# Chunk mask of the prompt attention: from separate one-row matmuls to two extra contraction rows

## The chip, the cores and the metric

The kernel runs on one core of a Trainium2 chip. The metric is the device time of one execution in microseconds (us). The kernel before takes 1581.94 us, the median of three runs (1581.4 to 1583.57).

## The reference

One layer of a streaming encoder on 1024 prompt positions and 8 x 16 sample positions. The change lies in the attention of the prompt (8 heads, 96 query and key values per head, chunks of 64 positions):

```
key_chunk = jnp.arange(S) // CHUNK                 # CHUNK = 64
q_chunk = (i * Q_BLOCK + jnp.arange(Q_BLOCK)) // CHUNK
s = jnp.einsum('bqhd,bkhd->bhqk', qi, k).astype(jnp.float32) * ATTN_SCALE
mask = key_chunk[None, :] <= q_chunk[:, None]
s = jnp.where(mask[None, None], s, NEG_INF)        # NEG_INF = -1e30
pr = jax.nn.softmax(s, axis=-1).astype(v.dtype)
return jnp.einsum('bhqk,bkhd->bqhd', pr, v)
```

Around it stand the input projection, the attention of the sample with its cache, a state-space layer, the output projection and a gated feed-forward part with a depthwise convolution. The S5, sample and feed-forward parts are not touched.

## The kernel before

All products are float32 made of pairs: an operand is split into a high part (written as float32r by ScalarE) and a low part (the rest, by VectorE or GpSimd), and `mm3` at L132 issues three matmuls, high by high, low by high and high by low.

The prompt attention is `phase_c` (L1120). The 1024 positions are four groups `j` of 256, each of two halves `z` of 128; the eight heads are two groups `g` of four. A stage is one (j, g), in the order j = 0, 1, 3, 2. The parts of a stage are generators that are advanced step by step:

- `back(i)` makes the keys of 128 positions: scale, transposes `ptk`, the split into `kh` and `kl` (tiles `kT[j]`). `kh` has 97 rows: 96 of the key and one row of ones, which a DMA on GpSimd's queue (L1159) brings from the array `one`.
- `prep(j, g)` (L1182) loads the queries from DRAM into `qnl`, transposes them into `ptq` and splits them into `qh` (97 rows) and `ql`. Both come from the pool of eight slots with the tag `L` (`wk`, L769), which they share with `cTh`, `cTl` (inputs of the projections of the next 128 positions), `O` (output of the attention) and the weights `ws`, `wh`, `wl`.
- `rowmax(j, g)` (L1196) finds the maximum of each query: matmuls of the high parts into `psm` (L1214), a reduction `mx` on VectorE (L1218), a transpose `pm`, and a copy of the negated maximum into row 96 of `qh` (L1227, ScalarE).
- `attn(j, g)` (L1232) takes one head and one `j` of the keys a step: three matmuls for each half of the keys into `pst` (L1247 with all 97 rows, so that the maximum is subtracted by the product; L1248; L1249), exponential `pf` (L1254), split into `ph` and `pl` (L1256, every third `pl` on GpSimd), and three matmuls each into `po` (L1260 to L1262).

Only the diagonal (keys of the same `j`) needs a mask: in each block of 128 by 128, the first 64 queries must not see the last 64 keys. Before, a further matmul adds -1e30 there. It has one contraction row in bfloat16, 128 stationary columns of `sel` (zeros and ones) and 64 moving columns of `neg`, at L1216 in `rowmax` and at L1251 in `attn`:

```
nc.tensor.matmul(p_[:, u, n - 64:n], lhsT=sel[:, 0], rhs=neg, start=False, stop=True)
nc.tensor.matmul(o_[:, 0:64], lhsT=sel[:, 1], rhs=neg, start=False, stop=True)
```

Each of the two lines issues 64 matmuls (8 stages, 4 heads, 2 halves). Four memsets on VectorE (L1134 to L1137) fill `sel` and `neg`.

`step` (L1319) interleaves the steps of `rowmax` and `attn`; the loop at L1330 mixes them with the projections (`middle`, `front`) of the later positions, and `phase_de` with the loads and the first matmuls `pw` of the output projection. Within this program order the framework writes the order of each engine's instructions itself (L1703, `schedule_with_timeline_sim=True`), from its own model of durations, and gives out the slots of the pools; only a part of the feed-forward has PE's order written by hand (L1582). On the chip every engine then runs its list in that order.

Of the kernel before, what the change touches and what calls it, by code (L numbers as in the profile page):

```python
# [10 lines left out]
F32R = mybir.dt.float32r  # L11
BF16 = mybir.dt.bfloat16
# [5 lines left out]
P = 128  # L18
# [9 lines left out]
H = 8  # L28
# [2 lines left out]
RD = 32  # L31
QN = 64
QD = QN + RD
NATW = QL + KL + RD
SW = 512
DIN = NATW + SW
# [16 lines left out]
NEG = -1e30  # L53
# [21 lines left out]
def build(tc, t):  # L75
    nc = tc.nc
# [3 lines left out]
    with root:  # L80
# [688 lines left out]
        def wk(tag, shape, name, dt=F32, rows=P):  # L769
            n = 1  # L770
            for z in shape:
                n *= z
            sz, bufs = {"L": (1024, NL), "M": (512, NM)}[tag]
            x = cst["W"].tile([P, sz], dt, tag=tag, name=name, bufs=bufs)[0:rows, 0:n]
            if len(shape) > 1:
                ax = "abcdef"[:len(shape)]
                x = x.rearrange("p (%s) -> p %s" % (" ".join(ax), " ".join(ax)), **dict(zip(ax[1:], shape[1:])))
            return x
# [341 lines left out]
        def phase_c():  # L1120
# [3 lines left out]
            kT, V = {}, {}  # L1124
            cst["V"] = V
            sc = cst["cw"]
            cs_ = cst["W"]
# [1 line left out]
            load(gq, t["g_qh"])  # L1129
            load(gk, t["g_kh"])  # L1130
            stt(gq, gq, SCALE, gk, ALU.mult, ALU.mult)
            sel = cs_.tile([1, 2, P], BF16, name="sel")
            neg = cs_.tile([1, 64], BF16, name="neg")
            nc.vector.memset(neg, NEG)  # L1134
            nc.vector.memset(sel, 0.0)
            nc.vector.memset(sel[:, 0, 0:64], 1.0)
            nc.vector.memset(sel[:, 1, 64:P], 1.0)  # L1137
            for j in range(4):
                es = ExitStack()
                kv = es.enter_context(tc.tile_pool(name=f"kv{j}", bufs=1, **R))  # L1140
                kvs.append(es)
                kT[j] = [kv.tile([QD + 1 - n, H, 2 * P], F32R, name=f"k{'hl'[n]}{j}") for n in range(2)]
                V[j] = [kv.tile([P, 2, H, QN + 1 - n], F32R, name=f"v{n}{j}") for n in range(2)]
                nc.gpsimd.memset(V[j][0][:, :, :, QN:QN + 1].bitcast(F32), 1.0)
            aps = ExitStack()
# [6 lines left out]
            def back(i):  # L1152
                j, z = i // 2, i % 2
                tsl = slice(i * P, (i + 1) * P)
                zs = slice(z * P, (z + 1) * P)
                kh, kl = kT[j]
                kn, qs, rr = pj.pop(i)
                if z == 0:
                    nc.gpsimd.dma_start(out=kh[QD:QD + 1].rearrange("p h q -> p (h q)"), in_=t["one"].bitcast(F32R))  # L1159
                rq = rr[:, 0].rearrange("p (h o) -> p h o", o=1)  # L1160
                rk = rr[:, 1].rearrange("p (h o) -> p h o", o=1)
                mul(kn[:, :, QN:QD], kpe[:, i:i + 1].to_broadcast([P, H, RD]), rk.to_broadcast([P, H, RD]), nc.gpsimd)
                for g in range(2):
                    h4 = slice(4 * g, 4 * g + 4)
                    mul(kn[:, h4, 0:QN], kn[:, h4, 0:QN], rk[:, h4].to_broadcast([P, 4, QN]))
                    pt = psum(TG[4] if i not in TE else TGE[2], [QD, 4, P], "ptk")
                    for h in range(4):
                        nc.tensor.transpose(pt[:, h], kn[:, 4 * g + h], ident)
                    split(kh[0:QD, h4, zs], kl[:, h4, zs], pt)
                cr = sc.tile([P, H, 16], F32, tag="cr", name="cr")  # L1170
                sr = sc.tile([P, H, 16], F32, tag="sr", name="sr")
                mul(cr, cosb[:, i:i + 1].to_broadcast([P, H, 16]), rq.to_broadcast([P, H, 16]), nc.gpsimd)
                mul(sr, sinb[:, i:i + 1].to_broadcast([P, H, 16]), rq.to_broadcast([P, H, 16]), nc.gpsimd)
                for g in range(2):
                    h4 = slice(4 * g, 4 * g + 4)
                    rope(sc, qs[g][:, :, QN:QD].rearrange("p h (a d) -> p h a d", a=2), qs[g][:, :, QN:QD], cr[:, h4], sr[:, h4], "rp", nc.gpsimd)
                    mul(qs[g][:, :, 0:QN], qs[g][:, :, 0:QN], rq[:, h4].to_broadcast([P, 4, QN]), nc.gpsimd)
                    store(q_dram[tsl, g * 4 * QD:(g + 1) * 4 * QD].rearrange("p (h d) -> p h d", d=QD), qs[g])
# [1 line left out]
            qT = {}  # L1180

            def prep(j, g):  # L1182
                qh = wk("L", [4, 2 * P], "qh", F32R, QD + 1)
                ql = wk("L", [4, 2 * P], "ql", F32R, QD)
                qT[j, g] = (qh, ql)
                for z in range(2):
                    zs = slice(z * P, (z + 1) * P)
                    qn = wk("M", [4, QD], "qnl")
                    i = 2 * j + z
                    load(qn, q_dram[i * P:(i + 1) * P, g * 4 * QD:(g + 1) * 4 * QD].rearrange("p (h d) -> p h d", d=QD))  # L1190
                    pt = psum(TG[5 if not pos["post"] else 10], [QD, 4, P], "ptq")
                    for h in range(4):
                        nc.tensor.transpose(pt[:, h], qn[:, h], ident)
                    split(qh[0:QD, :, zs], ql[:, :, zs], pt, gq)

            def rowmax(j, g):  # L1196
                qh, _ = qT[j, g]
                nb = j // 2 + 1
                mx = cs_.tile([P, 4, 2, 2], F32, tag="mx", name="mx", bufs=2)
                nm = cs_.tile([P, 4, 2], F32, tag="nmx", name="nmx", bufs=2)  # L1200
                for c in range(2):
                    for h in (2 * c, 2 * c + 1):
                        for z in range(2):
                            lh = qh[0:QD, h, z * P:(z + 1) * P]
                            for hb in range(nb):
                                tot = 0
                                p_ = psum(TG[6], [P, 2, 2 * P], "psm")
                                for u in range(2):
                                    jj = 2 * hb + u
                                    if jj > j:  # L1210
                                        break
                                    n = P if jj == j and z == 0 else 2 * P
                                    dg = jj == j
                                    nc.tensor.matmul(p_[:, u, 0:n], lhsT=lh, rhs=kT[jj][0][0:QD, 4 * g + h, 0:n], start=True, stop=not dg)  # L1214
                                    if dg:
                                        nc.tensor.matmul(p_[:, u, n - 64:n], lhsT=sel[:, 0], rhs=neg, start=False, stop=True)  # L1216
                                    tot += n
                                nc.vector.tensor_reduce(out=mx[:, h, z, hb:hb + 1], in_=p_.rearrange("p a k -> p (a k)")[:, 0:tot],  # L1218
                                                        axis=AX.X, op=ALU.max)
                                if (h % 2, z, hb) != (1, 1, nb - 1):  # L1220
                                    yield
                    nc.vector.tensor_reduce(out=nm[:, 2 * c:2 * c + 2], in_=mx[:, 2 * c:2 * c + 2, :, 0:nb], axis=AX.X, op=ALU.max, negate=True)
                    pm = psum(TG[7], [1, 2, 2, P], "pm")
                    for hh in range(2):
                        for z in range(2):
                            nc.tensor.transpose(pm[:, hh, z], nm[:, 2 * c + hh, z:z + 1], ident)
                    acopy(qh[QD:QD + 1, 2 * c:2 * c + 2], pm.rearrange("p h z q -> p h (z q)"))  # L1227
                    yield
# [3 lines left out]
            def attn(j, g):  # L1232
                qh, ql = qT.pop((j, g))
                O = wk("L", [4, 2 * P], "O", rows=QN + 1)
                for h in range(4):
                    po = psum("y", [QN + 1, 2 * P], "po")
                    for jj in range(j + 1):
# [6 lines left out]
                        for z, (sc_, qs_) in enumerate(cols):  # L1244
                            ks = slice(z * P, (z + 1) * P)
                            o_ = p_[:, sc_]
                            nc.tensor.matmul(o_, lhsT=kh[:, 4 * g + h, ks], rhs=qh[:, h, qs_], start=True, stop=False)  # L1247
                            nc.tensor.matmul(o_, lhsT=kl[:, 4 * g + h, ks], rhs=qh[0:QD, h, qs_], start=False, stop=False)  # L1248
                            nc.tensor.matmul(o_, lhsT=kh[0:QD, 4 * g + h, ks], rhs=ql[:, h, qs_], start=False, stop=not dg)  # L1249
                            if dg:  # L1250
                                nc.tensor.matmul(o_[:, 0:64], lhsT=sel[:, 1], rhs=neg, start=False, stop=True)  # L1251
                        pf = wk("M", [4 * P], "pf")
                        ph, pl = [cst["ap"].tile([P, 4 * P], F32R, tag=x_, name=x_) for x_ in ("ph", "pl")]
                        nc.scalar.activation(out=pf[:, 0:n], in_=p_[:, 0:n], func=AF.Exp)  # L1254
# [368 lines left out]
def arrays(inp):  # L1623
# [3 lines left out]
    o = {}  # L1627
    x = np.concatenate([a["x_prompt"].reshape(SEQ, DM), a["x_sample"].reshape(NB * DSEQ, DM)], 0)
    o["xT"] = c(x.T)
    o["one"] = np.ones((1, 2 * P * H), f)  # L1630
    o["ident"] = np.eye(P, dtype=f)
    pos = np.concatenate([np.arange(SEQ), np.tile(PAST + np.arange(DSEQ), NB)]).astype(f)
    inv = (f(10000.0) ** (-np.arange(0, RD, 2, dtype=f) / f(RD))).astype(f)
# [91 lines left out]
```

## Time and profile before

| | |
|---|---|
| median of the timed runs | 1581.94 us |
| span of the profiled execution | 1582.0 us (the page gives no other time of it) |
| PE busy | 1497.2 us (95%) |
| PE weight loads busy | 1427.5 us (90%) |
| VectorE (DVE) busy | 1119.5 us (71%) |
| ScalarE (ACT) busy | 683.8 us (43%) |
| GpSimd (POOL) busy | 320.6 us (20%) |
| mask matmuls, L1216 and L1251 | 64 each, 435.6 to 656.7 us |

PE is TensorE's matmul row, PEld its weight loads. The duration of a matmul in the profile holds its passage through the array, so that matmuls that follow each other overlap in the rows; what one takes of the engine is the distance between its start and the start of the next.

### The profile page before, as it was taken

Reading aid. Unit: us, or ns where it says so; the run is one execution under the profiler, and the core shown is the slowest. Engines: PE = TensorE matmul, PEld = TensorE weight load, DVE = VectorE, ACT = ScalarE, POOL = GpSimd, SP = SyncE. Lnnn points to the kernel's source line nnn. Section 1 sums busy time; section 2 is a strip of 40 time slices with the busy share of each in tenths; the row PEclk is TensorE's granted clock in tenths of the full one; section 3 lists DMA queues with packets and bytes.
Section 4 is the critical chain, followed back from the end, with each engine's and each line's share of the span. In section 5 each row is a group of like instructions: output and inputs, shape, how many; then the busy total and the mean of one; then the engine's idle time right before and its main releaser. Section 6 shows DMA issues by size and latency. Waiting matters only on the chain.

```text
span 1582.0 us, 24076 instructions
## 1 busy us (share of the span) xinstructions
PE 1497.2 (95%) x8861; PEld 1427.5 (90%) x8861; DVE 1119.5 (71%) x2376; ACT 683.8 (43%) x1323; POOL 320.6 (20%) x616
## 2 busy tenths in 40 slices
PE   7896857999999999999999999999999999999998
PEld 6876745877888898999999999999999999999998
DVE  8983799485777676367676766776766777777766
ACT  6442346666666676434433333333333333333321
POOL 3550466130444222112100000000100000000000
PEclk9998867999999999999999999999999999999999
DMA  7449343463321222451021111111111111111103
GB/s 203 122 144 161 114 154 57 111 186 97 97 69 48 78 65 65 151 165 52 1 84 37 41 41 41 50 45 40 41 41 41 46 49 51 44 41 40 41 1 130
DMA packets 101205, 122.00 MB, mean 77 GB/s; under 512 B 39240, under 2 KB 81416, under 8 KB 100624
## 3 DMA queue, kind: packets, MB, share of 16 engines
q1 hardware_dynamic: 100960, 120.44, 27.1%
q8 instruction: 69, 1.13, 0.3%
q14 instruction: 48, 0.39, 0.1%
q0 software_dynamic: 128, 0.03, 0.0%
HBM read 93.79 MB, written 26.65 MB: 76 GB/s over the span
## 4 chain that ended last, share of the span: by engine, by line
PE 80%; DVE 11%; DMA 4%; ACT 2%; issue 1%; SPq 1%; POOL 0%; DVEq 0%; ACTq 0%
PE pu L137 35%; PE pd L137 16%; PE pw L137 6%; DVE w L104 3%; PE pk L137 3%; PE pst L1247 2%; PE pg L137 1%; PE pq L137 1%; PE psm L1214 1%; PE pst L1248 1%; PE po L1260 1%; PE po L1262 1%; PE pst L1249 1%; PE pS L137 1%; PE po L1261 1%
## 5 line engine op out<-in xcount | busy, mean ns | idle before, releaser
L104 DVE TENSOR_TENSOR hT<-hT,pd 128x384 f32<-128x384 f32 x528 | 288.2, 551 | 211.7 <-PE pd L137 211.6
L137 PE MATMUL pu<-hnh,wl 128*128 128x384 f32 x1056 | 353.9, 335 | 0.0
L137 PE MATMUL pu<-hnl,wh 128*128 128x384 f32 x1056 | 353.9, 335 | 0.0
L137 PE MATMUL pu<-hnh,wh 128*128 128x384 f32 x1056 | 353.6, 335 | 0.0
L137 PE MATMUL pd<-act,wh 128*128 128x384 f32 x1056 | 348.0, 336 | 0.5 <-DVE hT L104 0.4
L1532 ACT ACTIVATE c<-pu,cvh 128x384 f32<-128x384 f32 x132 | 88.7, 672 | 302.1 <-PE pu L137 302.0
L137 PEld LDWEIGHTS pd<-act,wh 128*128 128x128 f32 x1056 | 197.7, 188 | 2.4 <-DVE hT L104 2.3
L137 PEld LDWEIGHTS pu<-hnh,wh 128*128 128x128 f32 x1056 | 198.2, 188 | 0.0
L137 PEld LDWEIGHTS pu<-hnl,wh 128*128 128x128 f32 x1056 | 198.2, 188 | 0.0
L137 PEld LDWEIGHTS pu<-hnh,wl 128*128 128x128 f32 x1056 | 198.0, 187 | 0.0
L122 DVE SCALAR_TENSOR_TENSOR c<-u,cvh,c 128x256 f32<-128x256 f32 (+1 forms) x352 | 171.1, 516 | 26.8 <-ACT u L101 13.8
L137 PE MATMUL pd<-act,wl 128*128 128x384 f32 x528 | 178.3, 338 | 0.0
L101 ACT ACTIVATE act<-c 128x384 fp32r<-128x384 f32 x66 | 34.7, 526 | 158.8 <-DVE c L104 158.8
L137 PEld LDWEIGHTS pd<-act,wl 128*128 128x128 f32 x528 | 99.2, 188 | 0.0
L1538 POOL COPY u<-u 128x2 f32<-128x2 f32 x88 | 20.0, 228 | 379.1 <-DVE c L104 172.1
L104 DVE TENSOR_TENSOR wl<-ws,wh 128x1024 fp32r<-128x1024 f32 x74 | 91.0, 1234 | 6.0 <-ACT wh L101 6.0
L101 ACT ACTIVATE wh<-ws 128x1024 fp32r<-128x1024 f32 x74 | 78.0, 1057 | 11.7 <-PE pw L137 6.5
L1550 POOL COPY cvo<-u 128x2 f32<-128x2 f32 x44 | 8.1, 184 | 353.9 <-ACT u L101 353.9
L1218 DVE TENSOR_REDUCE mx<-psm 128x1 f32<-128x512 f32 (+2 forms) x96 | 52.3, 550 | 29.8 <-PE psm L1216 15.0
L1554 ACT ACTIVATE c<-c 128x384 f32<-128x384 f32 x66 | 34.7, 526 | 75.1 <-DVE c L122 75.0
L101 ACT ACTIVATE u<-pu 128x384 f32<-128x384 f32 (+2 forms) x176 | 66.2, 404 | 0.0
L137 PE MATMUL pw<-oh,wh 128*128 128x384 f32 x192 | 64.9, 339 | 0.0
(468 smaller groups left out, 3174.6 us busy)
## 6 DMA issues: line engine op xcount, KB each, us to landing
ws<-in_w_up SPq DMA_DIRECT2D x44, 512.0 KB, 3.7
ws<-in_w_down SPq DMA_DIRECT2D x22, 512.0 KB, 3.6
xs<-in_xT SPq DMA_DIRECT2D x24, 192.0 KB, 3.5
os<-o_dram SPq DMA_DIRECT2D x24, 192.0 KB, 2.7
hT<-in_xT SPq DMA_DIRECT2D x24, 192.0 KB, 4.3
out_yT<-hT SPq DMA_DIRECT2D x24, 192.0 KB, 2.1
cf<-in_cT SPq DMA_DIRECT2D x8, 512.0 KB, 4.7
cn<-in_cn SPq DMA_DIRECT2D x8, 512.0 KB, 7.1
```

The source lines that it names most:

```text
L101: nc.scalar.activation(out=out, in_=in_, func=AF.Copy, scale=scale)
L104: (eng or nc.vector).tensor_tensor(out=out, in0=a, in1=b, op=op)
L122: nc.vector.scalar_tensor_tensor(out=out, in0=a, scalar=s, in1=b, op0=op0, op1=op1)
L137: nc.tensor.matmul(out, lhsT=w, rhs=x, start=first and i == 0, stop=last and i == n - 1)
L1214: nc.tensor.matmul(p_[:, u, 0:n], lhsT=lh, rhs=kT[jj][0][0:QD, 4 * g + h, 0:n], start=True, stop=not dg)
L1218: nc.vector.tensor_reduce(out=mx[:, h, z, hb:hb + 1], in_=p_.rearrange("p a k -> p (a k)")[:, 0:tot], axis=AX.X, op=ALU.max)
L1247: nc.tensor.matmul(o_, lhsT=kh[:, 4 * g + h, ks], rhs=qh[:, h, qs_], start=True, stop=False)
L1248: nc.tensor.matmul(o_, lhsT=kl[:, 4 * g + h, ks], rhs=qh[0:QD, h, qs_], start=False, stop=False)
L1249: nc.tensor.matmul(o_, lhsT=kh[0:QD, 4 * g + h, ks], rhs=ql[:, h, qs_], start=False, stop=not dg)
L1532: nc.scalar.activation(out=c, in_=p_, func=AF.Identity, scale=w[2], bias=w[3])
L1538: nc.gpsimd.tensor_copy(out=u[:, 0:2], in_=halo[i, gv][:, TB:TB + 2])
L1554: nc.scalar.activation(out=g_, in_=g_, func=AF.Silu)
```

## The change

The constant row of the keys becomes three rows, and the queries get two rows more, so that the product of the two new pairs of rows is -1e30 for the masked combinations and 0 elsewhere. The tiles `kh` and `qh` have 99 rows (`QM`). Rows 96 to 98 of `kh` come by the same DMA on GpSimd's queue from the array `kmask` (3 x 2048 instead of 1 x 2048 values). For `qh`, each `prep` issues a new DMA on GpSimd's queue from `qmask` (3 x 1024 values) into rows 96 to 98; row 96 is zero until `rowmax` writes the negated maximum there. On the diagonal, `rowmax` and the first matmul of `attn` contract 99 rows; elsewhere they contract 96 and 97 as before. The matmuls with `sel` and `neg`, these tiles and their memsets are gone.

```diff
+QM = QD + 3
-            sel = cs_.tile([1, 2, P], BF16, name="sel")
-            neg = cs_.tile([1, 64], BF16, name="neg")
-            nc.vector.memset(neg, NEG)
-            nc.vector.memset(sel, 0.0)
-            nc.vector.memset(sel[:, 0, 0:64], 1.0)
-            nc.vector.memset(sel[:, 1, 64:P], 1.0)
...
-                kT[j] = [kv.tile([QD + 1 - n, H, 2 * P], F32R, name=f"k{'hl'[n]}{j}") for n in range(2)]
+                kT[j] = [kv.tile([(QM, QD)[n], H, 2 * P], F32R, name=f"k{'hl'[n]}{j}") for n in range(2)]
...
-                    nc.gpsimd.dma_start(out=kh[QD:QD + 1].rearrange("p h q -> p (h q)"), in_=t["one"].bitcast(F32R))
+                    nc.gpsimd.dma_start(out=kh[QD:QM].rearrange("p h q -> p (h q)"), in_=t["kmask"].bitcast(F32R))
...
-                qh = wk("L", [4, 2 * P], "qh", F32R, QD + 1)
+                qh = wk("L", [4, 2 * P], "qh", F32R, QM)
+                nc.gpsimd.dma_start(out=qh[QD:QM].rearrange("p h q -> p (h q)"), in_=t["qmask"].bitcast(F32R))
...
-                                    nc.tensor.matmul(p_[:, u, 0:n], lhsT=lh, rhs=kT[jj][0][0:QD, 4 * g + h, 0:n], start=True, stop=not dg)
-                                    if dg:
-                                        nc.tensor.matmul(p_[:, u, n - 64:n], lhsT=sel[:, 0], rhs=neg, start=False, stop=True)
+                                    r = QM if dg else QD
+                                    nc.tensor.matmul(p_[:, u, 0:n], lhsT=qh[0:r, h, z * P:(z + 1) * P], rhs=kT[jj][0][0:r, 4 * g + h, 0:n], start=True, stop=True)
...
-                            nc.tensor.matmul(o_, lhsT=kh[:, 4 * g + h, ks], rhs=qh[:, h, qs_], start=True, stop=False)
+                            r = QM if dg else QD + 1
+                            nc.tensor.matmul(o_, lhsT=kh[0:r, 4 * g + h, ks], rhs=qh[0:r, h, qs_], start=True, stop=False)
                             nc.tensor.matmul(o_, lhsT=kl[:, 4 * g + h, ks], rhs=qh[0:QD, h, qs_], start=False, stop=False)
-                            nc.tensor.matmul(o_, lhsT=kh[0:QD, 4 * g + h, ks], rhs=ql[:, h, qs_], start=False, stop=not dg)
-                            if dg:
-                                nc.tensor.matmul(o_[:, 0:64], lhsT=sel[:, 1], rhs=neg, start=False, stop=True)
+                            nc.tensor.matmul(o_, lhsT=kh[0:QD, 4 * g + h, ks], rhs=ql[:, h, qs_], start=False, stop=True)
...
+    for z in range(2):
+        km[1 + z, :, z, 1] = 1.0
+        qm[1 + z, :, z, 0] = NEG
```

## Rows read from the trace of the kernel before

**Rows 1.** The page: busy time, and PE's busy tenths in 40 slices.

```profile
PE 1497.2 (95%) x8861; PEld 1427.5 (90%) x8861; DVE 1119.5 (71%) x2376; ACT 683.8 (43%) x1323; POOL 320.6 (20%) x616
...
PE   7896857999999999999999999999999999999998
```

**Rows 2.** Instructions of L1251 and L1216 by line: ns min/median/max, first and last start.

```profile
L1251 PE MATMUL pst<-neg,sel x64: 197/198/198, 443.9 to 656.7; 1*128 1x64 bf16 x64
...
L1216 PE MATMUL psm<-neg,sel x64: 197/198/198, 435.6 to 635.8; 1*128 1x64 bf16 x64
```

**Rows 3.** Windows: busy us (instructions) of PE, PEld, DVE, ACT, POOL; clock, DMA, GB/s.

```profile
415.00:433.00 18.00, 18.00 (x107) 16.44 (x105) 17.21 (x51) 12.69 (x28) 12.52 (x28) 1.00 0.27 86
433.00:443.00 10.00, 7.72 (x49) 5.45 (x47) 9.81 (x30) 6.25 (x12) 5.74 (x14) 1.00 0.47 145
443.00:533.00 90.00, 90.00 (x629) 78.06 (x630) 64.24 (x160) 57.78 (x119) 38.91 (x73) 1.00 0.18 53
533.00:580.00 47.00, 46.18 (x366) 42.09 (x364) 34.71 (x55) 35.92 (x64) 10.27 (x7) 1.00 0.29 88
580.00:663.00 83.00, 83.00 (x622) 76.18 (x621) 44.16 (x78) 50.08 (x97) 14.82 (x11) 1.00 0.27 80
```

**Rows 4.** PE's timeline in an attention step on the diagonal: start us, us, instruction.

```profile
470.03 0.28 PE L1247 MATMUL pst<-qh,kh 97*128 97x256 f32 x1
470.15 0.28 PE L1248 MATMUL pst<-qh,kl 96*128 96x256 f32 x1
470.27 0.28 PE L1249 MATMUL pst<-ql,kh 96*128 96x256 f32 x1
470.48 0.20 PE L1251 MATMUL pst<-neg,sel 1*128 1x64 bf16 x1
470.61 0.33 PE L1247 MATMUL pst<-qh,kh 97*128 97x128 f32 x1
470.77 0.28 PE L1248 MATMUL pst<-qh,kl 96*128 96x128 f32 x1
470.88 0.28 PE L1249 MATMUL pst<-ql,kh 96*128 96x128 f32 x1
```

**Rows 5.** PE's timeline around a mask matmul of rowmax.

```profile
592.14 0.28 PE L1214 MATMUL psm<-kh,qh 96*128 96x256 f32 x1
592.36 0.20 PE L1216 MATMUL psm<-neg,sel 1*128 1x64 bf16 x1
592.49 0.39 PE L1247 MATMUL pst<-qh,kh 97*128 97x256 f32 x1
592.71 0.28 PE L1248 MATMUL pst<-qh,kl 96*128 96x256 f32 x1
```

**Rows 6.** PE's longest wait in 430 to 665 us: total us, times, longest.

```profile
PE psm L1214 <- ACT qh L101: 1.5, 3, 0.8
```

**Rows 7.** The DMA of the row of ones, L1159, on GpSimd: issue ns; landing us.

```profile
L1159 POOL DMA_DIRECT2D kh<-in_one x4: 484/487/669, 412.0 to 413.7; - x4
...
DMA to landing us min/median/max: 1.8/1.8/2.0
```

**Rows 8.** ScalarE's write of the queries' high part, by tile qh.

```profile
L101 ACT ACTIVATE qh<-ptq,gq x16: 668/682/686, 434.6 to 603.4; 96x512 fp32r<-96x512 f32 x16
```

**Rows 9.** Windows of the instructions on tile sel: PE, PEld, DVE; clock, DMA, GB/s.

```profile
443.00:533.00 90.00, 12.46 (x63) 5.70 (x63) 0.00 (x0) 1.00 0.18 53
533.00:580.00 47.00, 4.55 (x23) 2.08 (x23) 0.00 (x0) 1.00 0.29 88
```

**Rows 10.** PE's timeline where a stage's first maximum waits for its queries.

```profile
534.17 0.48 PE L1214 MATMUL psm<-kh,qh 96*128 96x256 f32 x2
535.47 0.45 PE L1214 MATMUL psm<-kh,qh 96*128 96x256 f32 x2 [0.82 <-ACT qh L101]
```

**Rows 11.** A held slot: PE's last po of a head, then ScalarE's timeline.

```profile
477.12 0.23 PE L1262 MATMUL po<-pl,v 128*65 128x128 f32 x1
...
483.08 0.65 ACT L101 ACTIVATE O<-po 65x256 f32<-65x256 f32 x2 [0.53 <-PE pv L137]
```

More of the change, by code (lines that the diff above doesn't have):

```diff
@@ L1203, in rowmax @@
                         for z in range(2):
-                            lh = qh[0:QD, h, z * P:(z + 1) * P]
                             for hb in range(nb):
@@ L1629, in arrays @@
     o["xT"] = c(x.T)
-    o["one"] = np.ones((1, 2 * P * H), f)
+    km, qm = np.zeros((3, H, 2, 2, 64), f), np.zeros((3, 4, 2, 2, 64), f)
+    km[0] = 1.0
+    for z in range(2):
+        km[1 + z, :, z, 1] = 1.0
+        qm[1 + z, :, z, 0] = NEG
+    o["kmask"] = km.reshape(3, H * 2 * P)
+    o["qmask"] = qm.reshape(3, 4 * 2 * P)
     o["ident"] = np.eye(P, dtype=f)
```

## The prediction

> **What bounds the kernel now.** I read the page first, then the windows over the prompt attention, then PE's timeline inside it, and last what PE waited for. On the page PE is busy 95% of the span, and its slices are nines from the eighth on, to the end [rows 1]; the reader should see that the loose part is the first fifth, before any line of the change runs. The mask matmuls lie between 435.6 and 656.7 us [rows 2]. The windows cover that stretch: from 443 to 533 and from 580 to 663 us PE is busy all the time (90.00 of 90, 83.00 of 83), from 533 to 580 us 46.18 of 47, at the full granted clock of 1.00; only from 433 to 443 us is there a hole (7.72 of 10), with DVE busy 9.81 [rows 3]. A full busy row does not prove a full engine, since durations overlap, so the starts have to be read: in an unmasked sequence 256 columns follow each other at 0.12 us (470.03, 470.15, 470.27) and 128 columns at 0.11 (470.77, 470.88) [rows 4]. PE's waits in the stretch are small: the longest, for `qh`, comes to 1.5 us in three times [rows 6]. So PE's own work sets the end, and what is taken out of PE between 443 and 663 us moves everything behind it.
>
> **What goes.** 64 + 64 mask matmuls [rows 2]. Each is drawn 0.198 us long, which is neither its price nor a bound for it. Its price is read from the starts of its neighbours. In attention [rows 4]: the matmul ahead starts at 470.27, the mask at 470.48, the next at 470.61, the one after at 470.77. From 470.27 to 470.77 is 0.50 us; the two real matmuls alone would take 0.12 + 0.11 = 0.23; the mask costs 0.27. In rowmax [rows 5]: 592.14 to 592.71 is 0.57, the two real ones 0.24, the mask costs 0.33. So the price has three parts: about 0.09 before (0.21 instead of 0.12: the mask does not start when its predecessor would be through), 0.13 from the mask's start to the next, and 0.05 to 0.10 after (the next one is slow to be followed). Its ends are 0.13, the mask's own step alone, if the delays around it belong to the place and stay, and 0.33: over 128, from 16.6 to 42.2 us. Of the two whole readings I take the lower, 0.27: it stands for the attention half, and half of the rowmax masks sit behind 128 columns, which no row here prices, where the upper reading is behind 256. 128 x 0.27 = 34.6 us.
>
> The Trainium skill would price this otherwise. Its page "TensorE: Matmul & The Clock Gate", section "Back-to-back issue gap", says that a matmul of up to 64 columns occupies the engine for about 60 cycles, an issue floor near 25 ns. By that, an estimate of 128 x 25 ns = 3.2 us would go. The trace does not agree: 130 ns lie between the mask's start and the next start [rows 4].
>
> The four memsets go from DVE some hundred us before the first mask, where they stand in nobody's way: nothing.
>
> **What is added to PE.** The diagonal matmuls contract 99 rows instead of 96 or 97. The trace holds both 96 and 97, at the same 0.12 us a step (L1247 at 470.03, L1248 at 470.15) [rows 4]. Three more rows on 96 could cost three times what one more shows, nothing to the 0.01 us that the starts resolve: I take 0, with an end of 0.03 x 128 = 3.8 us.
>
> **What is added to GpSimd and the DMA.** Four row-of-ones DMAs become three rows wide, eight DMAs for `qh` are new. An issue takes GpSimd 0.48 to 0.67 us [rows 7], 8 x 0.49 = 3.9 us, beside 38.91 busy of 90 us and then 10.27 of 47 and 14.82 of 83 [rows 3]: hidden. If it were not, and each sat ahead of a `pl` that PE waits for, 3.9 us.
>
> The new wait: the first diagonal `psm` of a stage needs the rows of `qmask`, and everything behind it on PE's queue waits with it; so does the copy of the maximum into row 96 on ACT's. It takes 0.49 + 1.8 = 2.3 us from the slot's release to landing [rows 7], if three rows land as fast as one. Beside it run two writes of `qh` by ACT, 2 x 0.68 = 1.4 us [rows 8], and the query load and the transposes ahead of them. Uncovered, 0.9 us a stage, 7.2 us over eight; covered, 0. GpSimd also waits in its own queue for the slot, with its `pl` splits, the keys and the rotated queries behind. I take 0, since by the code the DMA waits for the slot alone, and ACT's writes for the query load and the transposes as well.
>
> **What is late next.** With the 63 masks from 443 to 533 us [rows 9] 17.0 us go from 90, leaving 73.0 against 64.24 us of DVE, 88%, and 57.78 of ACT; from 533 to 580 (23 masks, 6.2 us) 40.8 are left against 35.92 of ACT and 34.71 of DVE; from 580 on ACT and DVE have 50.08 and 44.16 us of 83, and nothing comes near. From 415 to 433 us DVE was at 17.21 of 18, 96%, and PE still at 18.00 [rows 3], so 88% is bearable. What I do expect is that stages begin with a short wait for their queries more often than now, as one does at 535.47 us, 0.82 us [rows 10], because the matmuls that covered the ACT and DVE steps are fewer, and because the order on each engine is written anew. I charge it to the four stages that begin between 443 and 533 us: 4 x 0.82 = 3.3 us. Its bounds are 0 and, with the uncovered 0.9 as well, 7.2 + 6 x 0.82 = 12.1 us.
>
> Sum: 34.6 - 3.3 = 31.3 us less. The profiled execution has a span of 1582.0 us, 0.06 from the median of the runs, so nothing is added for what lies around it: 1582.0 - 31.3 = **1550.7 us**.
>
> **Rivals.**
>
> *Half of it stays in the projections' stretch.* From 443 to 533 us the products of the later positions, keys and queries all pass DVE, ACT and GpSimd in order; if DVE's chain paces this stretch as soon as PE is a little faster, its 17.0 us are not gained: 1582.0 - 34.6 + 17.0 = 1564.4. For it: DVE at 9.81 of 10 right before [rows 3]. Against it: PE without a hole in all of the 90 us.
>
> *Only the mask's own step goes.* The delays around the mask may come from what follows (a new PSUM tile and its wait) and stay: 128 x 0.13 = 16.6, 1565.4. Against it: an ordinary L1247 of 256 columns is followed at 0.12 (470.03) [rows 4], the one behind the mask at 0.22 (592.49) [rows 5].
>
> *A mask costs little more than its columns.* By the pace of 256 columns in 0.12 us, 64 are 0.03, 3.8 us in all, less the 3.3 of new waits: 1581.5, no change. The neighbours' starts speak against it [rows 4, 5]. The section of the skill named above says the same with its 25 ns: by its estimate 1578.8 before any new wait.
>
> *Slower: the new DMA ties GpSimd's queue to the slots.* The eight slots are short: a head's last `po` starts at 477.12 us, and its copy into `O` comes at 483.08, when a projection (`pv`) has let go of a slot [rows 11], about 5.9 us. If each of the eight DMAs sits in GpSimd's queue for 5.9 us and then takes 2.3, less the 1.4 of ACT that run beside it, and PE has nothing else in order, that is 6.8 x 8 = 54 us: 1582.0 - 34.6 + 54 = 1601. It turns slower from 34.6 / 8 = 4.3 us of PE idle a stage. Against it: during that very hold PE had no hole, and from 533 us on GpSimd is busy less than a quarter [rows 3].
>
> **How the numbers follow.** Forecast 0.62, half in the stretch 0.17, own step only 0.07, no change 0.04, slower 0.07; the last 0.03 is for an order that loses some other 15 to 30 us. Range: below, 34.6 us go with no new wait, and the waits of now (2.28 and 0.82 us of PE's holes from 433 to 580 us) go too, 37.7, or the price is above 0.27 a piece: 1543. Above, the rival of the stretch with 6 x 0.82 us of waits on top, 1564.4 + 4.9, some 1570. Faster by more than 0.2% (3.2 us, about what a measurement of this kernel can tell from none): 0.62 + 0.17 + 0.07 and half of the last 0.03, 0.88; within it 0.05; slower 0.07.
>
> **What would show it.** PE: no bfloat16 matmul left, 128 instructions fewer, and 0.12 or 0.11 us between the starts of the diagonal `pst` matmuls where 0.50 lay over two. The 99-row ones at the same pace. The last `pst` near 626 us instead of 656, and the time from there to the end unchanged at about 925 us; if it grows, the gain was given back behind the attention. The `qmask` DMAs landed before the first `psm` of their stage; a wait of `psm` or of ACT's `qh` for a DMA of over 4 us a stage would be the slower rival, DVE above 96% from 443 us on the rival of the stretch. The forecast is wrong if the step from a real matmul to the next on the diagonal stays above 0.2 us, or if PE's holes between 433 and 663 us grow from 3 to over 15 us.

## The result, and the profile after

The changed kernel takes 1564.88 us (median of 4 runs, 1562.87 to 1569.64) against 1582.76 (1581.4 to 1583.63) of the kernel before on the same chip: a ratio of 0.9891 [0.9874, 0.9907], 17.9 us less. The forecast was 1550.7, so 57% of the expected gain came. The profiled execution has a span of 1563.1 us, 18.9 less than before.

The page after, busy time and PE's slices, beside [rows 1]:

```profile
PE 1470.5 (94%) x8733; PEld 1416.5 (91%) x8733; DVE 1114.7 (71%) x2372; ACT 680.1 (44%) x1323; POOL 328.3 (21%) x624
...
PE   6896866999989999999999999999999999999998
```

128 matmuls and four memsets are gone, and GpSimd has eight instructions more. PE's timeline in an attention step on the diagonal, after, beside [rows 4] (start us, duration us, instruction):

```profile
444.44 0.28 PE L1242 MATMUL pst<-qh,kh 99*128 99x256 f32 x1
444.55 0.28 PE L1243 MATMUL pst<-qh,kl 96*128 96x256 f32 x1
444.68 0.28 PE L1244 MATMUL pst<-ql,kh 96*128 96x256 f32 x1
444.79 0.23 PE L1242 MATMUL pst<-qh,kh 99*128 99x128 f32 x1
444.86 0.27 PE L1243 MATMUL pst<-qh,kl 96*128 96x128 f32 x1
444.97 0.27 PE L1244 MATMUL pst<-ql,kh 96*128 96x128 f32 x1
```

From the third start to the fifth lie 0.18 us where 0.50 lay, and the 99 rows are followed as fast as 96. The windows of the attention after, beside [rows 3] (busy us and instructions of PE, PEld, DVE, ACT, POOL; clock, DMA, GB/s):

```profile
433.00:443.00 10.00, 5.77 (x37) 4.33 (x38) 9.12 (x28) 5.30 (x9) 7.80 (x18) 1.00 0.39 124
443.00:533.00 90.00, 86.23 (x658) 80.53 (x656) 72.19 (x176) 65.17 (x136) 42.15 (x75) 0.98 0.22 65
533.00:580.00 47.00, 46.06 (x398) 44.95 (x397) 37.47 (x59) 39.09 (x72) 13.98 (x11) 1.00 0.28 84
580.00:633.00 53.00, 52.11 (x411) 50.28 (x411) 30.40 (x59) 35.84 (x70) 10.62 (x8) 1.00 0.29 82
```

PE now has 9.8 us without a running matmul from 433 to 633 us; it had 3.1 from 433 to 663. That understates it, because a matmul's duration overlaps the next. So I counted in starts: for each matmul the time to the next start, less the step that its shape has in unbroken sequences (0.118 us for 256 columns, 0.174 for 384, 0.231 for 512, 0.03 for a mask by the pace of 256 columns). In the attention's products the step of 128 columns lies between 0.06 and 0.11 us, by what stands beside it; counting 0.06 for the matmuls of `psm` and for the first of `pst`, the price of the masks and the new holes below both come out some 2.5 us larger, their difference the same. What is left over is called excess below, and where no mask is involved, holes. It is taken from the last `pv` of the fourth position to the first `pu` of the feed-forward ("attention" below) and from there to the end:

```
                attention us   excess: masks   holes   feed-forward   last pst to end
before             315.2           34.0         6.1        1.8            925.3
after              290.1            0          18.8        8.3            933.2
```

The masks cost 34.0 + 128 x 0.03 = 37.8 us. New holes took 12.7 of them, the feed-forward 6.5, and 0.5 was gained ahead of the attention: -37.8 + 12.7 + 6.5 - 0.5 = -19.1, the change of PE's last start to 0.1. So two losses had to be explained. PE's waits after, from 425 to 665 us (total us, times, longest), beside [rows 6]:

```profile
PE pm L1220 <- DVE nmx L1216: 2.3, 2, 1.6
PE ptq L1189 <- DMA qnl<-q_dram: 1.9, 2, 1.6
PE po L1253 <- ACT ph L102: 0.9, 1, 0.9
PE po L1255 <- DVE pl L105: 0.8, 2, 0.5
PE psm L1210 <- ACT qh L102: 0.7, 1, 0.7
```

These five come to 6.6 us, mostly on VectorE and ScalarE, where the waits that the same view lists for before come to 3.1. And the new DMA after, by line (duration ns; what GpSimd waited for in it; who waited for it; landing us):

```profile
L1181 POOL DMA_DIRECT2D qh<-in_qmask x8: 541/563/566, 434.5 to 563.3; - x8
...
  PE pst L1244: 5.7, 1
  PE psm L1210: 4.0, 1
who waited for it (us, times):
  PE psm L1210: 0.2, 1
...
DMA to landing us min/median/max: 2.0/2.2/3.2
```

GpSimd did stand still for a slot, for 5.7 and 4.0 us, but PE waited for a `qmask` only once, 0.2 us. That was at the first stage, where PE's timeline shows a longer wait just ahead (the last `pv`, a transpose of the queries, the first `psm`):

```profile
432.48 0.40 PE L138 MATMUL pv<-wkvl,cTh 128*128 128x512 f32 x1
436.39 0.61 PE L1189 MATMUL ptq<-ident,qnl 128*96 128x128 f32 x4 [1.57 <-DMA qnl<-q_dram]
437.18 0.47 PE L1210 MATMUL psm<-kh,qh 99*128 99x128 f32 x2 [0.18 <-DMA qh<-in_qmask]
```

### The profile page after: what moved, and what is told of

Its sections match the earlier page's. It is cut to its first block, busy times and chain, and to the rows that moved or that the text cites. A ratio compares the mean times of both kernels' runs of the same rounds, so it can differ in the third digit from the quotient of the medians.

```text
span 1563.1 us, 23843 instructions
## 1 busy us (share of the span) xinstructions
PE 1470.5 (94%) x8733; PEld 1416.5 (91%) x8733; DVE 1114.7 (71%) x2372; ACT 680.1 (44%) x1323; POOL 328.3 (21%) x624
## 4 chain that ended last, share of the span: by engine, by line
PE 76%; DVE 13%; DMA 5%; ACT 2%; issue 2%; SPq 2%; POOL 0%; DVEq 0%; ACTq 0%; POOLq 0%
PE pu L138 36%; PE pd L138 17%; PE pw L138 6%; DVE w L105 3%; PE pk L138 2%; PE pg L138 1%; PE pq L138 1%; PE po L1255 1%; SPq L96 1%; PE pst L1242 1%; PE pst L1243 1%; PE pst L1244 1%; PE po L1254 1%; PE po L1253 1%; DMA U<-u_dram 1%
## 5 line engine op out<-in xcount | busy, mean ns | idle before, releaser
L1547 ACT ACTIVATE c<-c 128x384 f32<-128x384 f32 x66 | 34.6, 525 | 74.8 <-DVE c L123 74.7
L138 PE MATMUL pw<-oh,wl 128*128 128x384 f32 x192 | 64.4, 336 | 0.0
```

The lines of the kernel that those rows point to most:

```text
L138: nc.tensor.matmul(out, lhsT=w, rhs=x, start=first and i == 0, stop=last and i == n - 1)
L1547: nc.scalar.activation(out=g_, in_=g_, func=AF.Silu)
```

## Experiments

Each ratio is to the kernel before on the same chip. The excess is counted as above:

```
            timed us   ratio [95%]               attention us  masks  holes  feed-forward
pad640      1559.71    0.9855 [0.9836, 0.9875]      294.1        0     22.8      1.8
nomask      1556.29    0.9829 [0.9807, 0.9852]      289.5        0     18.1      1.8
both        1589.25    1.0045 [1.0029, 1.0061]      322.3       34.3   12.8      1.8
bshift      1588.42    1.0039 [1.0028, 1.0050]      315.0       34.0    5.7      8.3
early       1557.21    0.9822 [0.9802, 0.9842]      289.3        0     18.0      1.8
f32rmask    1603.45    1.0117 [1.0101, 1.0134]      327.3       52.1 together    8.3
plead10     1557.80    0.9827 [0.9806, 0.9849]      290.8        0     19.4      1.8
mrows       1563.25    0.9872 [0.9854, 0.9891]      294.5       10.3    9.0      1.8
plhalf      1555.41    0.9826 [0.9810, 0.9842]      288.2        0     16.9      1.8
m64         1583.07    1.0001 [0.9991, 1.0011]      315.4       34.3    5.9      1.8
m65         1564.59    0.9885 [0.9870, 0.9900]      294.2       10.4    8.6      1.8
```

**pad640: the changed kernel, with 640 bytes put back.** In the built programs the pool `W` and the pools of the feed-forward's weights lie 640 bytes (a partition) higher than before, because `sel` (512) and `neg` (128) are gone from `W`. A longer `gq` puts the weights back where they were before; every engine's order stays.

```diff
-            gq, gk = cs_.tile([QD, 1], F32, name="gq"), ...
+            gq, gk = cs_.tile([QD, 161], F32, name="gq")[:, 0:1], ...
```

> The changed kernel with one tile of the pool W made 640 bytes longer, the size of the two tiles that the change took out; the order on every engine is that of the changed kernel. Theory placement: the feed-forward part of the changed kernel is some 6.5 us slower than before because everything in W and the weights beside it moved by 640 bytes; with the bytes back its pd and pu steps return to those of before and the time is 1564.9 - 6.5 = 1558.4 us. Rival, the loss comes with the new instruction stream: 1564.9 us and the slow steps stay.

The feed-forward's excess fell from 8.3 to 1.8 us. The groups of `pu` from 800 to 1550 us, and the last one of `pd`, by line (busy us, mean ns of one | idle before), first of the changed kernel, then of pad640:

```profile
L138 PE MATMUL pu<-hnl,wh 128*128 128x384 f32 x956 | 322.8, 338 | 0.0
L138 PE MATMUL pu<-hnh,wl 128*128 128x384 f32 x955 | 322.1, 337 | 0.0
L138 PE MATMUL pu<-hnh,wh 128*128 128x384 f32 x952 | 321.8, 338 | 0.0
L138 PE MATMUL pd<-act,wl 128*128 128x384 f32 x472 | 158.6, 336 | 0.0
```

```profile
L138 PE MATMUL pu<-hnl,wh 128*128 128x384 f32 x956 | 320.4, 335 | 0.0
L138 PE MATMUL pu<-hnh,wl 128*128 128x384 f32 x955 | 320.1, 335 | 0.0
L138 PE MATMUL pu<-hnh,wh 128*128 128x384 f32 x952 | 318.9, 335 | 0.0
L138 PE MATMUL pd<-act,wl 128*128 128x384 f32 x483 | 163.2, 338 | 0.0
```

Same instructions, same order. The three groups of `pu` are 2 to 3 ns longer in the changed kernel, and so are the distances between their starts (1.8 to 2.8 ns over 3166 matmuls, 7.0 us); of `pd`, one group takes 1.1 us more and the one shown 1.5 us less. Together these are the 6.5 us.

**bshift: the kernel before, with `sel` and `neg` in another pool.** The converse: the masks stay, and `W` loses the 640 bytes. The keys and values move by as much; nine matmuls of the projections change place on PE, none in the feed-forward.

```diff
-            sel = cs_.tile([1, 2, P], BF16, name="sel")
-            neg = cs_.tile([1, 64], BF16, name="neg")
...
+                if j == 0:
+                    sel = kv.tile([1, 2, P], BF16, name="sel")
+                    neg = kv.tile([1, 64], BF16, name="neg")
```

> The kernel before with sel and neg in the pool of the first keys instead of W, so that W and the weights move by 640 bytes as in the changed kernel; masks as before. Theory placement: the steps of pd and pu become those of the changed kernel and the time grows by some 6.5 us to 1589 us. Rival, instruction stream: 1582.8 us and the steps of before.

Slower by 0.39%, with 8.3 us of excess in the feed-forward and the attention unchanged. From both sides, the placement is shown; in the table, every kernel with the 640 bytes in `W` has 1.8 us there and the two without 8.3, as the changed kernel has. Why these addresses are dearer, and those of which tile, was not found out; only the two placements were tried.

**nomask: the kernel before without its masks** (the mask is left out of the computation). It separates the removal from the extra rows and DMAs.

```diff
-                                    if dg:
-                                        nc.tensor.matmul(p_[:, u, n - 64:n], lhsT=sel[:, 0], rhs=neg, start=False, stop=True)
...
-                            if dg:
-                                nc.tensor.matmul(o_[:, 0:64], lhsT=sel[:, 1], rhs=neg, start=False, stop=True)
```

> The kernel before without the 128 mask matmuls: the mask is left out of the computation, nothing is put in its place; sel and neg and their memsets stay, so that the placement is that of before. Theory removal: the new holes of the attention (some 10 us against the 3 before) come because the covering matmuls are gone and the order is written anew, not from the new DMAs; the time is that of pad640, 1558 us. Rival, the qmask DMA makes the holes: without it they stay at those of before and the time is 1582.8 - 34.6 = 1548 us.

It gains 26.4 us, not 35 to 38: 18.1 us of holes are there without any new DMA or row. So most of the new holes belong to the removal itself, with the new order that comes with it. PE's waits in nomask, from 425 to 665 us:

```profile
PE psm L1214 <- ACT qh L101: 1.3, 3, 0.7
PE po L1258 <- DVE pl L104: 1.3, 2, 1.0
PE pm L1224 <- DVE nmx L1220: 1.0, 2, 0.7
PE psm L1214 <- DVE mx L1216: 1.0, 2, 0.6
```

**both: the changed kernel, with the old masks added** (on top of the rows; they change nothing in the values).

```diff
+                                    if dg:
+                                        nc.tensor.matmul(p_[:, u, n - 64:n], lhsT=sel[:, 0], rhs=neg, start=False, stop=True)
```

> The changed kernel with the mask matmuls, sel and neg kept as well, so that the mask is applied twice: the kernel before plus the 99 rows and the eight DMAs. Theory removal: 1582.8 us, within 3 us; a step of the 99-row matmuls equals one of 96 rows. Rival, the DMA and its wait cost the holes: 1582.8 + 8 = 1591 us.

My expectation missed: rows and DMAs cost 0.45%, 7 us, of which 6.7 are unmasked holes (12.8 against 6.1). 5.4 us more excess than before lies between 425 and 455 us: the first `psm` comes 4.6 us after the last `pv` where it came 2.3 after it before, and the granted clock stands at 1.2 GHz from 436 to 439 and from 442 to 449 us.

**early: pad640, with the `qmask` DMAs of the first two stages issued ahead of the loop.** In pad640 GpSimd's timeline shows the first `qmask` in the queue behind the products of the position that was just projected (start us, duration us):

```profile
429.67 1.18 POOL L105 TENSOR_TENSOR qs<-qs,rrc 128x256 f32<-128x256 f32 x2
430.79 0.57 POOL L1181 DMA_DIRECT2D qh<-in_qmask  x1
```

```diff
+            for st_ in stages[:2]:
+                qE[st_] = qopen()
...
-                qh = wk("L", [4, 2 * P], "qh", F32R, QM)
+                qh = qE.pop((j, g)) if (j, g) in qE else qopen()
```

(`qopen` holds the tile and its DMA, as `prep` did.)

> pad640 with one move: the slots of qh and the qmask DMAs of the first two stages are issued ahead of the loop over the projections instead of in prep. In pad640 and both the first psm comes 4.7 us after the last pv of the fourth 128 positions, where it is 2.3 us in before, nomask and bshift, and the granted clock falls to 0.5 for 3.4 us twice around it. Theory queue: the DMA came late because it stands in GpSimd's queue behind the products of the keys and queries; now the first psm is at 2.3 us again, the clock does not fall there, and the time is that of nomask, 1556.3 us. Rival, the three rows themselves or the tracking of row 96 delay it: 1559.7 us and 4.7 us.

The first `psm` is back at 2.4 us behind the last `pv`, and the holes at 18.0, what nomask has:

```profile
427.80 0.40 PE L138 MATMUL pv<-wkvl,cTh 128*128 128x512 f32 x1
430.21 0.31 PE L1215 MATMUL psm<-kh,qh 99*128 99x128 f32 x1
```

The order on PE was written anew here as well: the third group of transposes, which stood ahead of the first `psm` in the changed kernel, now stands behind it. With placement and first DMA mended, the extra rows cost nothing that can be measured: 0.9822 against 0.9829 of nomask, whose matmuls stand in the same order but for five places. The profile of pad640 also shows the clock at its lower level, 1.2 GHz, right behind the late start (window and columns as above; 0.75 is the mean granted clock):

```profile
433.00:443.00 10.00, 7.64 (x36) 5.95 (x36) 7.33 (x23) 4.89 (x9) 7.59 (x19) 0.75 0.13 43
```

In the changed kernel it fell only at 483 us, after three holes of 0.7 to 1.0 us in a row, up to 487; in nomask nowhere. Pad640's attention started 3.7 us earlier than that of the changed kernel (the stretch ahead varies by some 4 us between executions) and ended within 0.3 us of it: what it had gained was lost again, hence 22.8 against 18.8. The likely place is the clock, at 1.2 GHz in three stretches (from 435, 441 and 482 us) against one; the count of holes holds what this costs.

**plead10: early, with the queries of a stage prepared further ahead** (`PLEAD` 10 instead of 7), which puts more of PE's real work between a step's last `pst` and its first `po`: 4.45 us against 4.13.

```diff
-PLEAD = 7
+PLEAD = 10
```

> early with PLEAD 10 instead of 7: the queries of a stage are prepared ten rowmax steps ahead. By the order written for PE, real work between the last pst of an attention step and its first po is 4.45 us in the mean, 4.13 in early and pad640, 3.91 plus three masks in before. Theory cover: the holes of some 18 us in the attention are there because the masks, which took more time on the chip than their columns, covered the steps of ACT and DVE; with 0.3 us more cover a step the holes shrink by a third or more, 1551 us. Rival, DVE and ACT pace the stretch: no change against early, 1556 us.

No gain, holes 19.4. That PE has too little of other work there is not supported, though 0.3 us a step is a small change.

**plhalf: early, with every second instead of every third `pl` on GpSimd.**

```diff
-  eng=nc.gpsimd if cnt[0] % 3 == 0 else None)
+  eng=nc.gpsimd if cnt[0] % 2 == 0 else None)
```

> The version with the first two stages' qmask DMAs issued ahead (early), with every second instead of every third pl split on GpSimd, so VectorE has some 27 splits fewer in the attention. Theory (the holes of 18 us that remain in PE between 430 and 720 us come from VectorE's share of the chains pf to pl and mx to nmx being late): holes fall below 12 us, time about 1551. Rival (GpSimd's split is slower, so the chain it carries is the late one, or the holes are in ScalarE's steps and the order): holes stay at 18 or grow, time 1557 to 1562.

Holes 16.9: the rival's side. VectorE made 40 splits instead of 54, so 14 fewer and not the 27 expected; the run speaks against these splits as the main cause of the holes and does not exclude them. By its median it is the fastest kernel run here (27.6 us below the one before), though 0.9826 cannot be told from early's 0.9822.

**f32rmask: bshift, with the masks in float32r.** What makes a mask of 64 columns cost 0.27 us? The first theory was the switch of data type between neighbours.

```diff
-                    sel = kv.tile([1, 2, P], BF16, name="sel")
+                    sel = kv.tile([1, 2, P], F32R, name="sel")
```

> bshift with sel and neg in float32r instead of bfloat16: the 128 mask matmuls stay, with the same rows and columns. Theory switch: the delays ahead of and behind a mask come from the change of type between bfloat16 and float32r, so that a mask now takes no more than the 0.11 us of a 128-column weight load; 1588.4 - 128 x (0.27 - 0.11) = 1568 us, some more with new holes. Rival, a one-row or 64-column matmul is slow among wide ones whatever its type: 1588 us.

PE's timeline around such a mask:

```profile
472.95 0.28 PE L1250 MATMUL pst<-ql,kh 96*128 96x256 f32 x1
473.17 0.29 PE L1252 MATMUL pst<-neg,sel 1*128 1x64 f32 x1
473.39 0.33 PE L1248 MATMUL pst<-qh,kh 97*128 97x128 f32 x1
473.55 0.28 PE L1249 MATMUL pst<-qh,kl 96*128 96x128 f32 x1
```

That theory fell: with one type throughout, the delays stayed (0.22 us ahead, 0.16 behind) and the mask's own step rose from 0.13 to 0.22 us. Against bshift a part of PE's order in the attention was written anew as well.

**mrows, m64, m65: the masks kept, on more rows.** `sel` and `neg` get 128, 64 or 65 rows, zeros outside row 0; each engine's order is that of before.

```diff
-            sel = cs_.tile([1, 2, P], BF16, name="sel")
-            neg = cs_.tile([1, 64], BF16, name="neg")
+            sel = cs_.tile([65, 2, P], BF16, name="sel")
+            neg = cs_.tile([65, 64], BF16, name="neg")
```

> The kernel before with its masks kept, but sel and neg filled on all 128 rows (zeros outside row 0), so a mask contracts 128 rows instead of one; order and placement as before. Theory (the 0.27 us of a mask come from its single contraction row among matmuls of 96 to 97): with 128 rows a mask costs about its own step and the delays of 0.09 and 0.05 us go, some 0.11 to 0.13 a mask, 128 x 0.14 = 18 us less, about 1565. Rival 1 (any narrow bfloat16 matmul costs this between wide float32r ones, whatever its rows): no change, 1582.7, and the starts stay at 0.21, 0.13, 0.16 us. Rival 2 (more rows cost more): slower.

> As the run with masks on 128 rows, but sel and neg have 64 rows (zeros outside row 0); order and placement as before. Theory (the delays come with a matmul whose contraction stands in another row group of the array than its neighbours' 96, 97 and 128 rows; 64 is still such a one): starts at 0.21, 0.13 and 0.16 us as with one row, time 1582 to 1583. Rival (the delays come from the one row alone, or shrink in proportion to the rows): near 1563, or halfway, 1573.

> As the run before it with one row more, 65. Theory (row group: 65 rows count as the same group as the neighbours' 96 and 97): starts at 0.12, 0.04 and 0.14 us as with 128 rows, time about 1563. Rival (the cost falls gradually with the rows): as with 64 rows within 1 us.

The same instruction on 128 rows instead of one takes 20 us from the kernel. PE's timeline around a mask, first m64, then m65:

```profile
473.56 0.28 PE L1249 MATMUL pst<-ql,kh 96*128 96x256 f32 x1
473.77 0.20 PE L1251 MATMUL pst<-neg,sel 64*128 64x64 bf16 x1
473.90 0.33 PE L1247 MATMUL pst<-qh,kh 97*128 97x128 f32 x1
```

```profile
473.41 0.28 PE L1249 MATMUL pst<-ql,kh 96*128 96x256 f32 x1
473.53 0.20 PE L1251 MATMUL pst<-neg,sel 65*128 65x64 bf16 x1
473.57 0.31 PE L1247 MATMUL pst<-qh,kh 97*128 97x128 f32 x1
473.72 0.27 PE L1248 MATMUL pst<-qh,kl 96*128 96x128 f32 x1
```

With 64 rows the mask starts 0.21 us after its predecessor and is followed after 0.13, exactly as with one row [rows 4]; with 65 it is 0.12 and 0.04. One row more is worth 18 us. So it is neither the type nor the single row, but on which side of 64 the contraction stands while the neighbours have 96 to 128 (on 1, 64, 65 and 128 rows; nothing between 1 and 64 was tried). By the Trainium skill, page "TensorEngine Tiling (Array Packing)", section "Tiling Modes", the array can be split into tiles of 64 or 32 rows, and a change of the mode drains the engine; that fits the step between 64 and 65 rows, though no run here shows which mode an instruction was in.

## Why the prediction came out as it did

**What bounds the kernel** was right: in `m65`, where nothing but the masks' time on PE changed, 23.6 us less of it moved the end by 17.8. **The price of a mask** was right: 37.8 / 128 = 0.295 us where I took 0.27. Between the two halves of a diagonal step it was even 0.32 (0.18 us from the third start to the fifth where 0.50 lay): I had charged 0.11 us to the 128 columns behind the mask, which take 0.07 without it. The first of its three parts, the delay ahead, was no property of the place, as the rival "only the mask's own step" had it: it vanished with the mask, and with the 65th row. The 25 ns of the Trainium skill ("TensorE: Matmul & The Clock Gate", "Back-to-back issue gap") come near only for a mask of 65 rows, whose own step is 0.04.

**99 rows and the memsets' work** cost nothing, as said. But the memsets' tiles were not free to lose: I followed their instructions and not their bytes. "The time from there to the end unchanged" is the first step that failed: 925.3 became 933.2, of which 6.5 us are the feed-forward's matmuls on moved tiles. It had been named as a sign, with no price.

**The new DMA** took 2.2 us from issue to landing. That it fits the 2.3 of the estimate is luck: the 1.8 us of [rows 7] count from the start of the issue, so the 0.49 of the issue were in them already, and three rows do not land as fast as one. The same line of the code for the keys took 1.8 us with one row and takes 3.3 with three:

```profile
L1154 POOL DMA_DIRECT2D kh<-in_kmask x4: 518/521/702, 411.4 to 413.2; - x4
...
DMA to landing us min/median/max: 2.9/3.3/3.7
```

In later stages the new DMA was covered. "Covered, 0" failed for the first stage: I counted from the slot's release, and the queue ahead of the issue, not the slot, was what made it late. It cost about 2.4 us of PE at the start, plus what the lower clock took in pad640 and both. In the changed kernel most of the wait is put down to the load of `qnl` (1.57 us at 436.39), since transposes stand ahead of the first `psm` in PE's order there; but `qmask` had landed only 0.1 us before that `psm` started at 437.18, so without them it could hardly have been earlier.

**What is late next** is the mis-sized term: 3.3 us forecast, 12.7 measured, just above its upper bound of 12.1. I had charged one known wait to four stages. Of those four only one begins with a hole of over 0.2 us (0.44 at 512 us). There are 23 of that size, on `nmx`, `ph`, `pl`, `qh` and loads: some 6 us in all around the first stage's beginning, up to 444 us, where before had 2.5, and the others spread. The runs say how they come. In m65, which keeps the order of before, 24 us less of PE's work brought only 2.5 us more of holes (8.6 against 6.1); its masks still occupy 10.4 us. Taking these away too (nomask) shortens the attention by 4.7 us, not by 10.4 and their own steps. The newly written orders without masks (after, nomask, early, plead10, plhalf) all lie at 288 to 291 us; pad640, with the order of after, lies at 294. That looks like a limit of the engines beside PE, which no run shows directly; a little more cover and 14 splits less on VectorE each left it as it was. Which chain sets it stays open, and an old order with no masks at all was not tried.

**The rival** that named 1564.4 hit the time and not the cause: VectorE was to be above 96% from 443 us on and is at 72.19 of 90, 80%. About half of the 34.6 us was indeed lost, but in two places, one of them the feed-forward. The slower rival's hold was real (5.7 us in GpSimd's queue) and harmless, since PE had other work in order. Of the other signs, the last `pst` came at 629.9 us instead of 626, and PE's time without a running matmul grew from 3.1 to 9.8 us, under the 15 that would have refuted the forecast.

## What to carry to other kernels

Before removing a small matmul, look at its rows: one whose contraction is at most 64 rows (1 and 64 were tried) among wide neighbours may cost several times its columns, and filling it up with zero rows to 65 gave 18 of the 26 us that leaving it out gives here, with nothing else changed. A tile that goes moves what lies behind it: compare addresses as well as instructions, and restore them before judging a change. Price a new DMA from what stands ahead of it in its queue, and when a saving is a good part of a stretch, expect some of it to come back as small waits, as 12.7 of 37.8 us did here.

## What the runs showed of the hardware that was not expected

- Between matmuls of 96 to 128 rows, a bfloat16 matmul of 64 columns costs 0.30 us on 1 or 64 contraction rows (37.8 / 128; m64: 34.3 / 128 + 0.03) and 0.11 on 65 or 128 (10.4 / 128 + 0.03).
- In float32r on one row its own step is 0.22 us instead of 0.13; the kernel is 0.8% slower than with bfloat16 at the same excess in the feed-forward (1.0117 against 1.0039), with a part of PE's order changed.
- A shift of `W` and the weight tiles by 640 bytes a partition makes most matmuls of 384 columns in the feed-forward 1 to 3 ns longer (`pu`: 335 to 338) and one group 2 ns shorter (`pd<-act,wl`: 338 to 336). It costs 6.5 us there, in the changed kernel as in the one before (bshift: 0.39% of the time).
- On GpSimd's queue a DMA of one row of 8 KB landed 1.8 us after its issue began, one of three such rows 3.3 us, one of three rows of 4 KB 2.2 us (medians).
- PE's granted clock, at 2.4 GHz throughout the attention before, fell to 1.2 GHz there in several kernels, in these behind holes of 0.7 to 1.8 us in PE (after: once, at 483 us; early: once, at 475; pad640: at 435, 441 and 482; both: at 436 and 442). Holes alone do not decide it: the changed kernel kept 2.4 GHz behind 1.7 and 1.8 us at 435 and 441 us, and nomask kept it throughout with 1.1 us at 478.
